# Stick-breaking attention: weights as differences of running products, or running products against differences of values

## The chip, the cores and the metric

One core of a Trainium2 chip runs the whole layer. The metric is the device time of one execution in microseconds; the time before is the median of three runs.

## What is computed

The layer has two branches, which are merged by gates, projected and normalised. The part that the change concerns is the attention, for 8 heads of width 64 and 1,024 positions:

```python
z = einsum('bthd,bshd->bhts', qb, kb) * scale
log_fail = where(causal, log_sigmoid(-z), 0.0)          # causal: s < t
later = cumsum(log_fail, axis=3, reverse=True) - log_fail
w = where(causal, exp(log_sigmoid(z) + later), 0.0)
outs.append(einsum('bhts,bshd->bthd', w, vb))
```

With beta = sigmoid(z), the weight of value s for query t is beta[t,s] times the product of (1 - beta[t,j]) over s < j < t. Let F[t,s] be the product of (1 - beta[t,j]) over s <= j < t, so that F[t,t] = 1. Then the weight is F[t,s+1] - F[t,s], and the sum over s of weight times value is also v[t] plus the sum over s <= t of F[t,s] times (v[s-1] - v[s]), with v[-1] = 0. The kernel before uses the first form, the kernel after the last.

The rest of the layer is an input projection of x (1,024 by 5,632), a convolution of width 31 with a layer norm, two projections of the branches, an output projection and a layer norm over the residual sum.

## The kernel before, in words

All products are float32 split into a high and a low part: each 128x128 by 512 product is three matmuls (`mm_piece`, L194 to L206: high by high, high by low, low by high). Weights arrive in pieces of 128x512 by SyncE's DMA queue (L284), and `split_weight` (L233) makes the two parts: ScalarE copies the high part (L235); the low part is made by VectorE (L237), by GpSimd (L239), or by a negated copy (L241) and an accumulating DMA of GpSimd's queue (L242).

The order of the instructions on every engine is worked out on the host, when the program is built, by a small planner, `Timeline` (L65). It holds a clock for TensorE and for the other engines, the cost of each operation, and a queue for each engine, from which the operation of the lowest priority number that is ready goes first. On the chip each engine runs its list in order and waits on semaphores. For DMAs the planner assumes fixed times: 3,000 ns for a load of 256 KB, 3,500 or 4,500 ns for larger ones, `W_LAND` = 3,000 ns after the issue of an accumulating one.

The stages, in order of TensorE's work:

1. The values v = x wv (L1145), all eight blocks of 128 positions at once in the eight banks of PSUM. `ev_v` (L1151) adds the bias into a half block `vraw` (VectorE), and splits it into `v` (ScalarE L1160, VectorE L1161). There are 128 positions on the partitions of each block.
2. The dense items (`run_dense`, L307) in the order of a hand-written list (L1073 to L1095): q and k of heads 0 and 1, the first pair of the convolution's inputs, q and k of 2 and 3, and so on. The attention (`Attention.step`, L827) is put between them: whatever it can do goes first, and dense matmuls fill the rest.
3. The pairs: ten pairs of dense columns by a seven-product scheme (`run_pairs`, L1023), with convolution and its layer norm on VectorE below them.
4. The branch projections (`ev_a`, `ev_c`), the output projection (L1292, L1307) and the final norm.

A unit of attention is a head and two blocks of 128 queries, with all keys before them. `emit_z` (L727) makes z in PSUM by two matmuls a chunk (L734, L735). ScalarE makes f = sigmoid(-z) (L742) and b = sigmoid(z) (L743). When a block of queries has all its chunks, VectorE runs a scan over f backwards (L749), which leaves F in f, with 1 on the diagonal from the constant `eyez`; then it multiplies b by F shifted by one (L752). The last column of b is set to zero by GpSimd (L724). `emit_t` (L758) transposes blocks of b on TensorE (L767), ScalarE and VectorE split the result into `wth` and `wtl` (L774, L775), and `emit_pv` (L781) multiplies them by the values (L790), with the high part of v in the first 64 rows of the result and the low part in the last 64. At the end of a unit ScalarE copies the low rows to `pvt` (L805), and VectorE adds both into the head pair's result `att` (L806). When both heads of a pair are done, the gate of the attention (`ev_zatt`, L430) multiplies `att`, which is stored to memory (`keep`, L444).

`slots` (L708) limits the blocks in work: at most `N_F` = 3 for f and `N_W` = 5 for b. The planner also counts the half blocks in use (`live["hf"]`, at most `N_HF` = 8), among them one for the bias `bvt` until the last block of v is done (L1165).

Of the kernel before, what the change touches and what calls it, by code (L numbers as in the profile page):

```python
# [14 lines left out]
P = 128  # L15
# [3 lines left out]
H = 8  # L19
# [14 lines left out]


N_BLK, N_HF, N_RAW, N_SPL = 43, 8, 2, 5

N_F, N_W = 3, 5

# [21 lines left out]

W_LAND = 3000


class Timeline:  # L65
# [5 lines left out]
    def __init__(self):  # L71
        self.t = 0.0
        self.free = {"A": 0.0, "V": 0.0, "G": 0.0}
        self.queue = {"A": [], "V": [], "G": []}
        self.events = []
        self.pe = deque()
        self.seq = 0
        self.now = 0.0

    def at(self, when, fn):  # L80
# [81 lines left out]
def layer_kernel(ctx: ExitStack, tc, xT, x, wv, wd, wa, wc, wo, vec, bv, lng, lnb, cst, out):  # L162
# [92 lines left out]
    def feed(loads=1 << 30):  # L255
        while True:
# [21 lines left out]
            if i < min(loads, len(pieces)):  # L278
                if isinstance(pieces[i], tuple):
                    stat["load"] += 1  # L280
                    continue
                if stat["raw"] < N_RAW:
                    r = wp.tile([P, HALF], F32, name=f"wr{i}", tag="wr", bufs=N_RAW)
                    nc.sync.dma_start(r, pieces[i])  # L284
                    raw[i] = (r, tl.t + 3000)
                    stat["load"] += 1
                    stat["raw"] += 1
                    continue
# [141 lines left out]
    def ev_zatt(p):  # L430
# [11 lines left out]
        return f  # L442

    def keep(key, src, cols=slice(0, S)):  # L444
# [3 lines left out]
        nc.sync.dma_start(kept[key][:, cols], src)  # L448
        n_kept[key] = n_kept.get(key, 0) + 1

    def back(key, name):
        t = blk(name)
        nc.sync.dma_start(t, kept[key])
        return t

    def split_att(p):
        a = back(("att", p), f"attb{p}")
        yield tl.now + 3500
# [59 lines left out]
    def make_cc(i):  # L518
# [3 lines left out]
        z = back(("c", ZCONV0 + i), f"zs{i}")  # L522
        yield tl.now + 3500
        cch[i], ccl[i] = blk(f"cch{i}", F32R), blk(f"ccl{i}", F32R)
# [182 lines left out]

    slots = {"f": 0, "w": 0}  # L708

    def alloc_unit(u):  # L710
        n = u.nslots
        ft = [blk(f"f{u.h}{u.m}{i}") for i in range(n)]
        bt = [blk(f"b{u.h}{u.m}{i}") for i in range(n)]
        slots["f"] += n
        slots["w"] += n
        if n == 1:
            u.f = [ft[0][:, 0:HALF], ft[0][:, HALF:S]]
            u.w = [bt[0][:, 0:HALF], bt[0][:, HALF:S]]
        else:
            u.f, u.w = [t[:, :] for t in ft], [t[:, :] for t in bt]  # L720
        for tb in range(2):

            last = P * (2 * u.m + tb + 1) - 1
            nc.gpsimd.memset(u.w[tb][:, last:last + 1], 0.0)  # L724
            tl.cost("G", tl.t, 0)

    def emit_z(u):  # L727
# [9 lines left out]
        c1 = min(c1, n)  # L737
        f, w = u.f[tb], u.w[tb]
        c2 = min(c1, n - 1)

        def g():
            yield act(0, f[:, c0:c1], ps[:, :c1 - c0], AF.Sigmoid, n=c1 - c0, scale=-SCALE)  # L742
            yield act(0, w[:, c0:c2], ps[:, :c2 - c0], AF.Sigmoid, n=c1 - c0, scale=SCALE)  # L743
            drop("ps")
            u.left[tb] -= 1
            if u.left[tb]:
                return

            yield ("V", 2, n, lambda: nc.vector.tensor_tensor_scan(  # L749
                f[:, 0:n][:, ::-1], f[:, 0:n][:, ::-1], eyez[:, S - n:S][:, ::-1], 0.0, op0=ALU.mult,  # L750
                op1=ALU.max), {"per": 2.083})
            u.ready[tb] = yield vtt(1, w[:, 0:n - 1], w[:, 0:n - 1], f[:, 1:n], ALU.mult, n)  # L752
            if u.nslots == 2 or u.ready[1 - tb] is not None:
                slots["f"] -= 1

        tl.spawn(g(), tl.t + 165)

    def emit_t(u):  # L758
# [22 lines left out]
    def emit_pv(u, i, wh, wl):  # L781
# [13 lines left out]
        if i == 0:  # L795
            p = h // 2
            if att[p] is None:
                att[p] = blk(f"att{p}")
            tmp = hf(f"pvt{h}{m}")
            r0 = (h % 2) * DH  # L800
            dst = att[p][r0:r0 + DH, m * 256:(m + 1) * 256].rearrange("p (b t) -> p b t", b=2)[:, ::-1, :]
# [18 lines left out]
    class Attention:  # L820
# [6 lines left out]
        def step(self):  # L827

            now = tl.t
            if self.pvq and self.pvq[0][0] is not None and self.pvq[0][0] <= now - GUARD and \  # L830
                    (self.pvq[0][1].ps is not None or live["ps"] < 7):
                emit_pv(*self.pvq.popleft()[1:])
                return True
            if self.zd and live["hf"] <= N_HF - 2 and live["ps"] < 7:
                u = self.zd[0]
                if all(r is not None and r <= now - GUARD for r in u.ready):
                    self.pvq.append(emit_t(u))
                    if not u.t:
                        self.zd.popleft()
                        slots["w"] -= u.nslots  # L840
                    return True
            if self.cur is None and self.wait:
                u = self.wait[0]
                if qk_ready[u.h] <= now and slots["w"] + u.nslots <= N_W and slots["f"] + u.nslots <= N_F:
                    self.cur = self.wait.popleft()
# [27 lines left out]
    def make_t(k):  # L873
# [3 lines left out]
        nc.sync.dma_start(rb, xT[k + NK // 2])  # L877
        yield tl.now + 4500
        a, b = blk(f"ta{k}"), blk(f"tb{k}")
# [21 lines left out]
    def make_s(n):  # L901
        c0, c1 = pairs[n]
        ra, rb = blk(f"rc{c0}"), blk(f"rc{c1}")
        nc.sync.dma_start(ra, wd[c0])
        nc.sync.dma_start(rb, wd[c1])
        while live["hf"] >= N_HF:
            yield tl.now + 200
        s = hf(f"s{n}")
        yield tl.now + 4500
        have = source[n] = {"A22": rb[:, hi_]}  # L910
# [19 lines left out]
    def split_operand(wh, wl, n, name, then):  # L930
# [4 lines left out]
        if name in DMA_LOW:  # L935
            yield act(1, wl, src, scale=-1.0)
            dsrc = wd[pairs[n][1]][:, hi_] if name == "A22" else src
            e = yield "G", 0, 0, lambda: nc.gpsimd.dma_start(wl, dsrc, accum_op=ALU.add), {"extra": 430}
            e += W_LAND
        else:  # L940
# [9 lines left out]
    def gate_out(t, c, half):  # L950
# [10 lines left out]
        keep(("c", c), t, cols)  # L961
        yield tl.now + 3000
        drop("hf")

    def pair_out(n, pp):
# [16 lines left out]
        nc.sync.dma_start(u, kept["p1", n][:, lo_])  # L982
        yield tl.now + 3000
        yield from add(u, "P6", u)
# [87 lines left out]

    qk_item(0)  # L1073
    qk_item(1)
    glu_item(0)
    qk_item(2)
    qk_item(3)
    glu_item(1)
    zatt_item(0)
    qk_item(4)  # L1080
    qk_item(5)
    zatt_item(1)
    qk_item(6)
    qk_item(7)
    p12_item(0)
    p12_item(1)
    zatt_item(2)
    att_done = lambda: flags["att"]
    z_done = lambda: heads_z_done(H - 1)
    glu_item(2, z_done)  # L1090
    glu_item(3, z_done)
    p12_item(2)
    zatt_item(3)
    for n in range(3, len(pairs)):
        p12_item(n)  # L1095
# [53 lines left out]
    tl.free["V"] = tl.t - 4000  # L1149

    def ev_v(tb):  # L1151
        while live["hf"] >= N_HF:
            yield tl.now + 100
        t = hf(f"vraw{tb}")
        vt[tb] = blk(f"v{tb}", F32R)
        v3 = vt[tb].rearrange("p (h e) -> p h e", h=H)
        t3 = t.rearrange("p (h e) -> p h e", h=H)
        yield vtt(0, t, vps[tb], bvt, ALU.add)
        drop("ps")
        yield "A", 0, HALF, lambda: nc.scalar.activation(v3[:, :, 0:DH], t3, AF.Copy)  # L1160
        yield "V", 1, HALF, lambda: nc.vector.tensor_tensor(v3[:, :, DH:P], t3, f32(v3[:, :, 0:DH]), op=ALU.subtract)  # L1161
        drop("hf")
        v_left[0] -= 1
        if v_left[0] == 0:
            drop("hf")  # L1165

# [10 lines left out]
    next(dense)  # L1177
    v_left = [NT]
    for tb in range(NT):
        tl.spawn(ev_v(tb), tl.t - (NT - 1 - tb) * 680 + 165)  # L1180
# [4 lines left out]
    def wo_stream():  # L1185
        for i in range(2 * NK):
# [5 lines left out]
            nc.sync.dma_start(r, src)  # L1192
            yield tl.now + 3000
            if i % 2 == 0:
# [198 lines left out]
```

## Time and profile before

| | |
|---|---|
| median of three runs | 768.82 us (767.13 to 770.05) |
| the profiled execution: its own time | 767.04 us |
| its span, first to last instruction | 765.0 us |
| TensorE busy | 748.2 us, 98% of the span |
| VectorE busy | 651.3 us, 85% |
| ScalarE busy | 379.7 us, 50% |
| GpSimd busy | 69.5 us, 9% |
| mean granted clock of TensorE | 0.994 |

A busy time is the time in which at least one instruction of the engine ran; the records of TensorE overlap, so its busy time says only when it stood still. A group's idle time is how long its engine stood idle just before its instructions, with what ended that wait. The DMA share of a stretch is the mean busy share of the core's 16 DMA engines.

### The profile page before, as it was taken

The page shows a single profiled execution, that of the slowest core. Times are in us where ns is not written, and L with a number is a line of the kernel's source. Part 1 is how long each engine was busy: PE and PEld are TensorE (multiplying, and loading weights), DVE is VectorE, ACT ScalarE, POOL GpSimd, SP SyncE. Part 2 cuts the span into 40 slices and gives each one's busy share as a digit, 9 for nine tenths or more (in the row PEclk, how much of TensorE's full clock was granted, in tenths as well). Part 3 has the DMA queues.
Part 4 walks back from the last instruction along what each step waited for, and adds up shares of the span by engine and source line. Part 5 has one row for each costly group of instructions (what it writes and reads, how often), then busy time and mean ns, then how long its engine had stood idle before and what let it go on. Part 6 is the DMA issues. An engine that isn't in the chain of part 4 may idle for free.

```text
span 765.0 us, 10211 instructions
## 1 busy us (share of the span) xinstructions
PE 748.2 (98%) x3622; PEld 625.4 (82%) x3622; DVE 651.3 (85%) x1006; ACT 379.7 (50%) x716; POOL 69.5 (9%) x132
## 2 busy tenths in 40 slices
PE   9999999999999999999999999999998999999995
PEld 7888888788888878888888888877786888888885
DVE  7554999999999999997999999999699859810985
ACT  2149965986388799844524433345472424200100
POOL 3311011101011011101100000000000023000000
PEclk9999999999999999999999999999999999999998
DMA  7525123412432224557725454453347876230052
GB/s 233 184 63 110 35 56 74 92 30 62 103 80 59 57 56 96 125 140 259 207 83 185 146 163 155 139 191 125 126 149 240 317 266 217 79 148 1 0 200 75
DMA packets 43394, 98.01 MB, mean 128 GB/s; under 512 B 4816, under 2 KB 5712, under 8 KB 43344
## 3 DMA queue, kind: packets, MB, share of 16 engines
q1 hardware_dynamic: 36864, 85.77, 33.5%
q0 software_dynamic: 6336, 11.54, 9.4%
q8 instruction: 28, 0.46, 0.3%
q14 instruction: 22, 0.18, 0.1%
q10 hardware_dynamic: 144, 0.07, 0.0%
HBM read 77.95 MB, written 19.40 MB: 127 GB/s over the span
## 4 chain that ended last, share of the span: by engine, by line
PE 58%; DVE 25%; ACT 9%; issue 6%; DMA 2%; SPq 0%; DVEq 0%; ACTq 0%
PE dps L203 11%; PE dps L198 11%; PE dps L199 11%; PE vps L1145 6%; DVE cacc L399 4%; PE yps L209 4%; PE yps L210 4%; PE yps L211 4%; PE pvps L790 3%; PE tps L767 3%; DVE cs L399 2%; DVE wl L396 2%; DVE c L396 2%; DVE cacc L396 2%; DVE u L396 2%
## 5 line engine op out<-in xcount | busy, mean ns | idle before, releaser
L198 PE MATMUL dps<-xh,wh 128*128 128x512 f32 x400 | 157.0, 393 | 0.0
L199 PE MATMUL dps<-xl,wh 128*128 128x512 f32 x400 | 156.0, 390 | 0.0
L203 PE MATMUL dps<-xh,wl 128*128 128x512 f32 x400 | 109.0, 391 | 0.0
L749 DVE TENSOR_TENSOR_SCAN f<-f,eyez 128x896 f32<-128x896 f32 (+3 forms) x64 | 85.0, 1343 | 5.1 <-ACT f L393 5.1
L235 ACT ACTIVATE wh<-wr 128x512 fp32r<-128x512 f32 x84 | 53.3, 634 | 72.4 <-DMA wr<-wv 25.5
L199 PEld LDWEIGHTS dps<-xl,wh 128*128 128x128 f32 x400 | 75.2, 188 | 14.2
L198 PEld LDWEIGHTS dps<-xh,wh 128*128 128x128 f32 x400 | 75.1, 188 | 14.3
L203 PEld LDWEIGHTS dps<-xh,wl 128*128 128x128 f32 x400 | 74.1, 188 | 14.6
L399 DVE SCALAR_TENSOR_TENSOR cacc<-cin,vecs,cacc 128x511 f32<-128x511 f32 (+14 forms) x116 | 82.4, 735 | 0.1
L242 POOL DMA_DIRECT2D wl<-wd x44 | 38.2, 868 | 271.7 <-ACT wl L241 240.8
L239 POOL TENSOR_TENSOR wl<-wr,wh 128x512 fp32r<-128x512 f32 x18 | 26.2, 1460 | 293.9 <-DVE wl L237 231.1
L210 PE MATMUL yps<-wol,mh 128*128 128x512 f32 (+1 forms) x136 | 51.2, 377 | 0.0
L211 PE MATMUL yps<-woh,ml 128*128 128x512 f32 (+1 forms) x136 | 51.2, 376 | 0.0
L209 PE MATMUL yps<-woh,mh 128*128 128x512 f32 (+1 forms) x136 | 51.2, 376 | 0.0
L396 DVE TENSOR_TENSOR wtl<-tps,wth 128x384 fp32r<-128x384 f32 (+1 forms) x80 | 46.7, 625 | 4.0 <-ACT wth L393 3.5
L399 DVE SCALAR_TENSOR_TENSOR xrow<-xrow,yps 128x512 f32<-128x512 f32 (+1 forms) x17 | 10.7, 653 | 43.0 <-PE yps L211 42.7
L393 ACT ACTIVATE f<-zps 128x384 f32<-128x384 f32 (+2 forms) x96 | 45.3, 515 | 3.8 <-PE zps L735 3.0
L393 ACT ACTIVATE wth<-tps 128x384 fp32r<-128x384 f32 (+1 forms) x80 | 40.2, 559 | 13.9 <-PE tps L767 13.2
L396 DVE TENSOR_TENSOR b<-b,f 128x895 f32<-128x895 f32 (+3 forms) x64 | 46.8, 743 | 0.3
L393 ACT ACTIVATE b<-zps 128x383 f32<-128x383 f32 (+2 forms) x96 | 46.2, 536 | 0.1
L399 DVE SCALAR_TENSOR_TENSOR cs<-cs,hs__77 128x511 f32<-128x511 f32 (+14 forms) x60 | 44.1, 735 | 0.1
L790 PE MATMUL pvps<-wtl,v 128*128 128x256 f32 (+1 forms) x160 | 39.7, 287 | 0.3 <-DVE wtl L396 0.2
(174 smaller groups left out, 1637.6 us busy)
## 6 DMA issues: line engine op xcount, KB each, us to landing
wr<-wd SPq DMA_DIRECT2D x60, 256.0 KB, 3.0
wl<-wd POOLq DMA_DIRECT2D x44, 256.0 KB, 4.6
rc<-wd SPq DMA_DIRECT2D x20, 512.0 KB, 5.6
c<-c SPq DMA_DIRECT2D x30, 256.0 KB, 3.1
ga<-c SPq DMA_DIRECT2D x8, 512.0 KB, 5.2
wor<-wo SPq DMA_DIRECT2D x16, 256.0 KB, 4.7
gc<-c SPq DMA_DIRECT2D x8, 512.0 KB, 6.3
xrow<-x SPq DMA_DIRECT2D x8, 512.0 KB, 5.8
```

Of the source, the lines that this page charges most:

```text
L198: nc.tensor.matmul(ps, wh[:, kk], mh, start=first and kk is ks[0], stop=False)
L199: nc.tensor.matmul(ps, wh[:, kk], ml, start=False, stop=False)
L203: nc.tensor.matmul(ps, wl[:, kk], mh, start=False, stop=last and kk is ks[3])
L209: nc.tensor.matmul(ps, wh, mh, start=first, stop=False)
L210: nc.tensor.matmul(ps, wh, ml, start=False, stop=False)
L211: nc.tensor.matmul(ps, wl, mh, start=False, stop=last)
L235: yield "A", 1, HALF, lambda: nc.scalar.activation(wh, r, AF.Copy)
L393: return "A", u, n, (lambda: nc.scalar.activation(out, in_, func, **kw)), (BIAS if "bias" in kw else {})
L396: return "V", u, n, lambda: nc.vector.tensor_tensor(out, a, b, op=op)
L399: return "V", u, n, (lambda: nc.vector.scalar_tensor_tensor(out, a, s, b, op0, op1)), (PTR if ptr else {})
L749: yield ("V", 2, n, lambda: nc.vector.tensor_tensor_scan(f[:, 0:n][:, ::-1], f[:, 0:n][:, ::-1], eyez[:, S - n:S][:, ::-1], 0.0, op0=ALU.mult,
L790: nc.tensor.matmul(u.ps[:, 0:n], st, wt[:, jj * 256:jj * 256 + n], start=(i == m and jj == 0 and wt is wh), stop=(i == 0 and jj == 1 and w ...
```

## The change

The kernel after transposes F itself, not b, and multiplies it by differences of values.

- In the attention: the second sigmoid, the multiplication by the shifted F and the zeroed column go. `N_F` becomes 6 and `N_W` goes. The scan's end is what the transposes wait for.
- In `ev_v`: the biased values stay in a block `vraw` (half t). A DMA of ScalarE's queue copies rows 0 to 126 of t to rows 1 to 127 of the other half, s; a second one brings the last row of the block before into row 0 (GpSimd sets a zero in the first block). TensorE transposes t in four matmuls, and four ScalarE copies put the result into `att`. VectorE makes s - t, which is then split as before. No value product is planned until all eight blocks are done.
- At the end of a unit ScalarE copies all 128 rows of the product to `pvt`, and two accumulating DMAs of GpSimd's queue add its two halves to `att`, one after the other (both write the same 64 rows).
- The planner gets one clock for all DMAs (`Timeline.dma`): each transfer takes its size at 250 bytes a ns after the ones before it, plus 2,000 ns; accumulating ones weigh 2.2 times. The copies of `ev_v` are not on that clock.
- The dense items follow a string, in which the convolution's third pair of inputs comes earlier (before the gate of head pair 1) and the fourth after the gate of pair 2; neither waits any more for all z to be done.
- The half block of `bvt` is no longer given back in the planner's count.

```diff
+ORDER = "q0 q1 g0 q2 q3 g1 z0 q4 q5 g2 z1 q6 q7 p2 z2 g3 p1 z3"
-N_F, N_W = 3, 5
+N_F = 6
-W_LAND = 3000
+DMA_RATE, W_ACC = 250, 2.2
...
+    def dma(self, kb, when=None, weight=1.0):
+        when = max(self.now, self.t) if when is None else when
+        self.dma_free = max(self.dma_free, when) + weight * kb * 1024 / DMA_RATE
+        return self.dma_free + 2000
...
-            e += W_LAND
+            e = tl.dma(256, e, W_ACC) + 500
...
-            yield act(0, w[:, c0:c2], ps[:, :c2 - c0], AF.Sigmoid, n=c1 - c0, scale=SCALE)
...
-            yield ("V", 2, n, lambda: nc.vector.tensor_tensor_scan(
+            u.ready[tb] = yield ("V", 2, n, lambda: nc.vector.tensor_tensor_scan(
...
-            u.ready[tb] = yield vtt(1, w[:, 0:n - 1], w[:, 0:n - 1], f[:, 1:n], ALU.mult, n)
...
-                    nc.tensor.transpose(ps[:, o:o + P], u.w[tb][:, j * P:(j + 1) * P], ident)
+                    nc.tensor.transpose(ps[:, o:o + P], u.f[tb][:, j * P:(j + 1) * P], ident)
...
-                yield act(0, tmp[0:DH, 0:256], u.ps[DH:P, 0:256], n=256)
-                yield vtt(0, dst, two(u.ps[0:DH, 0:256]), two(tmp[0:DH, 0:256]), ALU.add, 256)
+                yield act(0, two(tmp[:, 0:256])[:, ::-1, :], two(u.ps[:, 0:256]), n=256)
                 drop("ps")
+                for part in (slice(0, DH), slice(DH, P)):
+                    e = yield "G", 1, 0, (lambda part=part: nc.gpsimd.dma_start(dst, tmp[part, 0:256],
+                                                                                accum_op=ALU.add)), {"extra": 430}
+                    yield tl.dma(64, e, W_ACC) + 2000
...
+        vraw[tb] = b = blk(f"vraw{tb}")
+        t, s = b[:, 0:HALF], b[:, HALF:S]
+        yield vtt(0, t, vps[tb], bvt, ALU.add)
+        drop("ps")
...
+        nc.scalar.dma_start(s[1:P, :], t[0:P - 1, :])
+        if tb:
+            nc.scalar.dma_start(s[0:1, :], vraw[tb - 1][P - 1:P, 0:HALF])
+        else:
+            nc.gpsimd.memset(s[0:1, :], 0.0)
...
+            for p in range(NC):
+                nc.tensor.transpose(ps[:, p * P:(p + 1) * P], t[:, p * P:(p + 1) * P], ident)
...
+        yield [act(1, att[p][:, tb * P:(tb + 1) * P], ps[:, p * P:(p + 1) * P], n=P) for p in range(NC)]
+        drop("ps")
+        yield tl.now + 1500
...
+        yield vtt(1, s, s, t, ALU.subtract)
+        yield "A", 0, HALF, lambda: nc.scalar.activation(v3[:, :, 0:DH], s3, AF.Copy)
+        yield "V", 1, HALF, lambda: nc.vector.tensor_tensor(v3[:, :, DH:P], s3, f32(v3[:, :, 0:DH]), op=ALU.subtract)
         v_left[0] -= 1
-        if v_left[0] == 0:
-            drop("hf")
```

## Rows read from the trace of the kernel before

**Rows 1.** The page: busy time, share of the span and instructions of each engine.

```profile
PE 748.2 (98%) x3622; PEld 625.4 (82%) x3622; DVE 651.3 (85%) x1006; ACT 379.7 (50%) x716; POOL 69.5 (9%) x132
```

**Rows 2.** Stretches: us, busy us of PE, PEld, DVE, ACT, POOL; clock, DMA share, GB/s.

```profile
60.00:80.00 20.00, 19.84 (x103) 16.63 (x102) 11.98 (x15) 19.70 (x40) 3.91 (x14) 1.00 0.51 106
...
220.00:240.00 20.00, 19.46 (x108) 16.66 (x107) 19.76 (x26) 19.67 (x44) 2.20 (x8) 1.00 0.24 53
260.00:280.00 20.00, 19.02 (x112) 15.82 (x110) 18.22 (x27) 19.50 (x41) 2.07 (x8) 1.00 0.28 54
...
520.00:540.00 20.00, 18.63 (x90) 15.34 (x90) 17.39 (x26) 12.03 (x19) 0.00 (x0) 1.00 0.54 169
580.00:600.00 20.00, 17.48 (x67) 13.31 (x67) 15.56 (x24) 5.46 (x9) 0.00 (x0) 0.91 0.92 326
```

**Rows 3.** Groups by line that the change removes or replaces.

```profile
L396 DVE TENSOR_TENSOR b<-b,f 128x895 f32<-128x895 f32 (+3 forms) x64 | 46.8, 743 | 0.3
L393 ACT ACTIVATE b<-zps 128x383 f32<-128x383 f32 (+2 forms) x96 | 46.2, 536 | 0.1
L396 DVE TENSOR_TENSOR att<-pvps,pvt 64x256 f32<-64x256 f32 x32 | 12.7, 407 | 1.4 <-ACT pvt L393 0.9
L724 POOL MEMSET b<- 128x1 f32 x64 | 8.8, 390 | 16.1 <-PE tps L767 12.1 <-DVE b L396 4.0
```

**Rows 4.** Groups by line nearest to what the change adds.

```profile
L767 PE MATMUL tps<-eyez,b 128*128 128x128 f32 x288 | 37.3, 273 | 1.7 <-DVE b L396 1.6
L1338 ACT ACTIVATE xrow<-xrow,st 128x128 f32<-128x128 f32 x1 | 0.4, 387 | 0.0
L242 POOL DMA_DIRECT2D wl<-wd x44 | 38.2, 868 | 271.7 <-ACT wl L241 240.8 <-PE dps L203 12.0 <-ACT f L393 6.7
```

**Rows 5.** The tile vraw: duration min/median/max in ns, first and last start in us.

```profile
L396 DVE TENSOR_TENSOR vraw<-vps,bvt x8: 681/691/692, 45.0 to 50.9; 128x512 f32<-128x512 f32 x8
L1160 ACT ACTIVATE v<-vraw x8: 615/624/633, 45.7 to 51.6; 128x512 fp32r<-128x512 f32 x8
L1161 DVE TENSOR_TENSOR v<-vraw,v x8: 680/684/685, 49.7 to 54.5; 128x512 fp32r<-128x512 f32 x8
```

**Rows 6.** DMA queues: packets, MB, time as a share of 16 engines' span.

```profile
q1 hardware_dynamic: 36864, 85.77, 33.5%
q0 software_dynamic: 6336, 11.54, 9.4%
q10 hardware_dynamic: 144, 0.07, 0.0%
```

**Rows 7.** DMA issues by line: count, KB each, median us to landing.

```profile
wr<-wd SPq DMA_DIRECT2D x60, 256.0 KB, 3.0
wl<-wd POOLq DMA_DIRECT2D x44, 256.0 KB, 4.6
```

**Rows 8.** Stretches of 5 us after the values, columns as in the second group.

```profile
50.00:55.00 5.00, 5.00 (x23) 4.13 (x22) 5.00 (x9) 3.00 (x6) 1.88 (x2) 1.00 0.60 144
55.00:60.00 5.00, 5.00 (x24) 4.13 (x22) 0.94 (x2) 4.67 (x8) 0.86 (x1) 1.00 0.83 183
60.00:65.00 5.00, 5.00 (x24) 4.13 (x22) 0.75 (x1) 4.88 (x9) 1.92 (x6) 1.00 0.90 182
65.00:70.00 5.00, 5.00 (x25) 4.13 (x24) 2.02 (x1) 4.97 (x12) 0.00 (x0) 1.00 0.37 68
70.00:75.00 5.00, 5.00 (x23) 4.13 (x22) 4.20 (x5) 4.90 (x11) 0.85 (x1) 1.00 0.07 18
```

**Rows 9.** Timeline, 67 to 79 us: start us, us, engine, line, operation; idle before.

```profile
67.44 2.02 DVE L749 TENSOR_TENSOR_SCAN f<-f,eyez 128x896 f32<-128x896 f32 x1 [5.06 <-ACT f L393]
...
76.23 1.42 PE L767 MATMUL tps<-eyez,b 128*128 128x128 f32 x11 [0.15 <-DVE b L396]
...
78.55 0.28 PE L790 MATMUL pvps<-wth,v 128*128 128x256 f32 x1
```

**Rows 10.** The tile tps: duration min/median/max in ns, first and last start in us.

```profile
L767 PE MATMUL tps<-eyez,b x288: 270/273/328, 76.2 to 336.0; 128*128 128x128 f32 x144
```

More of the change, by code (lines that the diff above doesn't have):

```diff
@@ L448, in keep @@
         nc.sync.dma_start(kept[key][:, cols], src)
+        tl.dma((cols.stop - cols.start) / 2)
         n_kept[key] = n_kept.get(key, 0) + 1
@@ L457, in split_att @@
         a = back(("att", p), f"attb{p}")
-        yield tl.now + 3500
+        yield landed[f"attb{p}"]
         ach[p], acl[p] = blk(f"ach{p}", F32R), blk(f"acl{p}", F32R)
@@ L522, in make_cc @@
         z = back(("c", ZCONV0 + i), f"zs{i}")
-        yield tl.now + 3500
+        yield landed[f"zs{i}"]
         cch[i], ccl[i] = blk(f"cch{i}", F32R), blk(f"ccl{i}", F32R)
@@ L712, in alloc_unit @@
         ft = [blk(f"f{u.h}{u.m}{i}") for i in range(n)]
-        bt = [blk(f"b{u.h}{u.m}{i}") for i in range(n)]
         slots["f"] += n
[L715 to L725, printed above, removed]
+        u.f = [ft[0][:, 0:HALF], ft[0][:, HALF:S]] if n == 1 else [t[:, :] for t in ft]
     def emit_z(u):
@@ L829, in step @@
             now = tl.t
-            if self.pvq and self.pvq[0][0] is not None and self.pvq[0][0] <= now - GUARD and \
+            if v_left[0] == 0 and self.pvq and self.pvq[0][0] is not None and self.pvq[0][0] <= now - GUARD and \
                     (self.pvq[0][1].ps is not None or live["ps"] < 7):
@@ L843, in step @@
                 u = self.wait[0]
-                if qk_ready[u.h] <= now and slots["w"] + u.nslots <= N_W and slots["f"] + u.nslots <= N_F:
+                if qk_ready[u.h] <= now and slots["f"] + u.nslots <= N_F:
                     self.cur = self.wait.popleft()
@@ L877, in make_t @@
         nc.sync.dma_start(rb, xT[k + NK // 2])
-        yield tl.now + 4500
+        yield tl.dma(1024)
         a, b = blk(f"ta{k}"), blk(f"tb{k}")
@@ L908, in make_s @@
         s = hf(f"s{n}")
-        yield tl.now + 4500
+        yield max(e, tl.now)
         have = source[n] = {"A22": rb[:, hi_]}
@@ L961, in gate_out @@
         keep(("c", c), t, cols)
-        yield tl.now + 3000
+        yield tl.dma_free + 2000
         drop("hf")
@@ L982, in pair_out @@
         nc.sync.dma_start(u, kept["p1", n][:, lo_])
-        yield tl.now + 3000
+        yield tl.dma(256)
         yield from add(u, "P6", u)
@@ L1071, in p12_item @@
         add_item(wd_src(pairs[n][0]), None, ev_p12(n), lambda: True, 1)
[L1073 to L1094, printed above, removed]
+    p12 = iter(range(len(pairs)))
+    for what in ORDER.split():
+        n = int(what[1:])
+        if what[0] == "q":
+            qk_item(n)
+        elif what[0] == "g":
+            glu_item(n)
+        elif what[0] == "z":
+            zatt_item(n)
+        else:
+            for _ in range(n):
+                p12_item(next(p12))
+    for n in p12:
         p12_item(n)
@@ L1149, in layer_kernel, with turn @@
     tl.free["V"] = tl.t - 4000
+    vraw = {}
     def ev_v(tb):
-        while live["hf"] >= N_HF:
-            yield tl.now + 100
-        t = hf(f"vraw{tb}")
+        vraw[tb] = b = blk(f"vraw{tb}")
+        t, s = b[:, 0:HALF], b[:, HALF:S]
+        yield vtt(0, t, vps[tb], bvt, ALU.add)
+        drop("ps")
+        raw_there.add(tb)
+        while tb and tb - 1 not in raw_there:
+            yield tl.now + 100
+        nc.scalar.dma_start(s[1:P, :], t[0:P - 1, :])
+        if tb:
+            nc.scalar.dma_start(s[0:1, :], vraw[tb - 1][P - 1:P, 0:HALF])
+        else:
+            nc.gpsimd.memset(s[0:1, :], 0.0)
+        got = []
+        def turn():
+            ps = bank("tps")
+            for p in range(NC):
+                nc.tensor.transpose(ps[:, p * P:(p + 1) * P], t[:, p * P:(p + 1) * P], ident)
+            tl.t += 4 * 109
+            got.append(ps)
+        yield turn
+        ps = got[0]
+        yield [act(1, att[p][:, tb * P:(tb + 1) * P], ps[:, p * P:(p + 1) * P], n=P) for p in range(NC)]
+        drop("ps")
+        yield tl.now + 1500
         vt[tb] = blk(f"v{tb}", F32R)
         v3 = vt[tb].rearrange("p (h e) -> p h e", h=H)
[L1157 to L1161, printed above, removed]
-        drop("hf")
+        s3 = s.rearrange("p (h e) -> p h e", h=H)
+        yield vtt(1, s, s, t, ALU.subtract)
+        yield "A", 0, HALF, lambda: nc.scalar.activation(v3[:, :, 0:DH], s3, AF.Copy)
+        yield "V", 1, HALF, lambda: nc.vector.tensor_tensor(v3[:, :, DH:P], s3, f32(v3[:, :, 0:DH]), op=ALU.subtract)
         v_left[0] -= 1
-        if v_left[0] == 0:
-            drop("hf")
+    raw_there = set()
     for i in range(NC):
@@ L1178, in layer_kernel @@
     v_left = [NT]
+    for p in range(NC):
+        att[p] = blk(f"att{p}")
     for tb in range(NT):
@@ L1192, in wo_stream @@
             nc.sync.dma_start(r, src)
-            yield tl.now + 3000
+            yield tl.dma(256)
             if i % 2 == 0:
```

21 lines of the change are left out of this document (10 added, 11 removed).

## The prediction

> **What bounds the kernel now.** I read the busy times first, then the stretches of 20 us, then the groups that the change touches. The reader is to see one thing in the first: TensorE is busy for 748.2 of 765.0 us [rows 1], so what VectorE and ScalarE save is worth time only where it ends a wait of TensorE. The stretches show how little of that there is. Of the 27 stretches between 60 and 600 us, ten hold idle time of TensorE of 0.05 us or more, the first at 60 to 80 and the last at 580 to 600, 6.8 us in all; the two largest outside the attention are 1.4 us at 520 to 540 and 2.5 us at 580 to 600, the latter with the granted clock at 0.91 (in part at 1.2 instead of 2.4 GHz), which costs 20 x 0.09 = 1.8 us more [rows 2]. So 8.6 us is about what can be won by taking waits away. The start, the output projection and the tail are not touched.
>
> The second thing is the stretch from 45 to 79 us. The values come out of PSUM from 45.0 us on and are split by 55.2 [rows 5]; the first scan starts at 67.4, the first transpose at 76.2, and the first value product at 78.6 [rows 9]. Some 23 us lie between the values being there and being wanted. VectorE is nearly idle in the middle of it, ScalarE is full from 55 on, and the DMA engines are 60 to 90% busy from 50 to 65 [rows 8]. The changed kernel puts its new steps here.
>
> **The change, part by part.**
>
> *Removed from the attention.* 96 second sigmoids, 46.2 us of ScalarE; 64 multiplications, 46.8 us, and 32 additions, 12.7 us, of VectorE; 64 memsets of GpSimd, 8.8 us [rows 3]. All of it lies beside TensorE's work. What it gives is shorter waits: the transposes' own waits for the multiplication are 1.6 us [rows 4], and VectorE, freed of 46.8 + 12.7 = 59.5 us less the 5.4 below, reaches the convolution's norm some 54 us sooner, so that this norm no longer competes with the operand splits before 540 and 600. I take the 5.7 us there (1.4 + 2.5 + 1.8) as won, and half of the other 2.9: 7.2 us. The bounds are 0 and 8.6.
>
> *Added to TensorE.* 8 x 4 transposes of t. 288 such cost 37.3 us of busy time [rows 4], 0.13 us each: 32 x 0.13 = 4.1 us, wholly on the path, since TensorE is the bound. The number of other matmuls is the same. Without the step below, the sum is 767.0 - 7.2 + 4.1 = 763.9 us.
>
> *Added to ScalarE and VectorE at the values.* 32 copies of 128 columns at up to 0.39 [rows 4], 12.4 us of ScalarE, and 8 differences at 0.68, 5.4 us of VectorE. ScalarE is full from 55 to 75 us [rows 8]; the copies take the place of about a quarter of the second sigmoids and delay q and k by a few us. I cost it at nothing because the four dense items ahead of heads 2 and 3, 4 x 48 matmuls at about 23 in 5 us [rows 8], are 42 us of work that stands ready; if it ran out, it would cost at most the 12.4.
>
> *Added to GpSimd's queue.* 64 accumulating DMAs, 64 x 0.87 = 56 us of issue [rows 4]. The second of each pair writes what the first writes and has to wait for its landing, 4.6 us where 256 KB are added [rows 7], and up to 32 x 4.6 = 147 us of that queue is waiting. The accumulations of weights stand behind it. Their pieces are split five ahead, so I cost it at nothing, and its failure is a rival. The planner's new DMA clock, the new order of the dense items and the half block that is not given back move no work of TensorE; I cost them at nothing within the bounds above.
>
> *The shift of the values.* This is the term that decides. Eight copies move 127 rows of 2 KB each from partition p to p + 1, on ScalarE's DMA queue, and VectorE's differences wait for them. No row shows such a copy. The lower bound is a load of 256 KB: 3.0 us [rows 7], hidden in the 23 us. For the upper bound, the queues' packets tell how rows are dealt: SyncE's queue has 256 transfers of 36,864 / 256 = 144 packets, which is 128 rows and one more for each of 16 engines; GpSimd's 44 have 6,336 / 44 = 144, and the one transfer of ScalarE's queue has 144 [rows 6]. So every transfer of this trace deals 8 whole rows to each of 16 engines. 127 rows can be dealt in equal whole shares only to one engine. If that is what happens, the rate is that of one engine: 85.77 MB in 0.335 x 16 x 765 = 4,100 us, 20.9 KB a us [rows 6]. Eight copies are 8 x 127 x 2,048 bytes = 2.08 MB, so 99.5 us on one engine, one behind the other.
>
> I take the upper end: the row nearest in size has 128 rows, but equal shares are what all 301 transfers show, and 127 has no other. The Trainium skill, on its page "DMA: Bandwidth & Descriptors" (section "Why a DMA increments its semaphore by 16 and not by 1"), says that a transfer runs on the largest number of engines up to 16 that divides the outer count of both sides, and names 127 partitions as a case of one; no run here shows it. The same page gives about 27 GiB/s for an engine, which would make the eight copies an estimated 72 us and my total about 819; the rows decide for the slower rate.
>
> Then the sum is this. The first copy can start when the first addition ends, 45.0 + 0.7 = 45.7 us [rows 5]. The engine also carries its share of the loads, by the DMA shares of 50 to 75 us 5 x (0.60 + 0.83 + 0.90 + 0.37 + 0.07) = 13.9 us [rows 8]; after that TensorE stands, and no more is asked for. The last copy lands at 45.7 + 99.5 + 13.9 = 159.1; difference, copy and low part take 0.68 + 0.62 + 0.68 [rows 5], so the values are there at 161.1. The first value product wants the last blocks, and wanted them at 78.6 [rows 9]. TensorE stands for 82.5 us. Nothing hides it: the list of TensorE is fixed, and VectorE, whose differences stand ahead of the scans and of the later heads' q, stands too and cannot work ahead. Total 763.9 + 82.5 = 846.4 against the profiled execution's own 767.0, which lies 1.8 below the median of the runs shown; within the width of this sum I leave that out and say 846.
>
> The bounds: at the fastest mean rate of any stretch shown, 326 / (16 x 0.92) = 22.1 KB a us [rows 2], and without other traffic, the values are there at 45.7 + 94.2 + 2.0 = 141.9, which makes 763.9 + 63.3 = 827; with the trace's mean share of traffic, 33.5 + 9.4 = 43% [rows 6], over all 100 us instead of the 13.9, they are there at 190 and the total is 875.
>
> **The rivals.**
>
> *The shift is spread over the engines* (0.29). Then it lands some 3 us after its issue, within the 23 us, and the total is 763.9, on the median's scale 766, with 758 to 773 for the bounds of idle time won (8.6 or 0). For it: the 3.0 us of the rows; nothing says that shares must be equal, a remainder could be dealt as well. Against it: no transfer in the trace has unequal shares. The same page of the Trainium skill reports an exception, rows dealt in rounded-up shares to all engines, for direct copies of GpSimd's queue; this copy is on ScalarE's. This case decides the sign: it holds if the copy lands within about 25 us for all eight, that is, on four engines or more.
>
> *The accumulations on GpSimd's queue are the wait* (0.06). The shift is quick, but each pair holds the queue for 0.87 + 4.6 + 0.87 = 6.3 us, 32 of them for 203 us of the 260 us of attention [rows 10], and the weights' low parts come up to 4.6 us late in places. If two or three of these land on TensorE, 764 + 9 to 14 = 773 to 778.
>
> *The shift is on one engine, and the first wait comes sooner* (within my case): if loads behind the copies are held up, TensorE stands from about 65 us on, some 14 us more than summed: 860.
>
> **How the numbers follow.** One engine: 0.65, forecast 846, its own range 825 to 875. Spread: 0.29, of which about half lies more than 0.5% below the median (0.5%, 3.8 us, is what a measurement of this kernel can tell from no change) and half within. GpSimd's queue: 0.06, slower for the most part. So faster 0.16, same 0.14, slower 0.70. Since both signs hold much of the chance, the range that holds 8 in 10 takes in most of the spread case: 760 to 875.
>
> **What would show it.** If I am right: in the DMA issues, the copies of vraw on ScalarE's queue take 12 us and more to land, the later ones near 100; in the waits, VectorE's difference (line of the helper, tile vraw) waits for that DMA some ten us at a time; a stretch between 75 and 150 us with hardly any TensorE; after it the stages as before. If the copies land in a few us and TensorE stays at 90% or more from 60 to 340 us, the rival holds and my forecast is wrong by the whole 82.5 us. VectorE's busy time falls by some 54 us either way, and 320 transposes take the place of 288. In the spread case the idle time at 520 to 600 should be gone; if it is still there, the freed time of VectorE was not what that wait wanted.

## The result, and the profile after

The kernel after takes 846.5 us (median of four runs, 845.22 to 847.30), the kernel before 767.98 in the same comparison: 1.1022 times as long, with an interval of 1.0985 to 1.1059. The forecast was 846. The total is right, but partly by luck: several of its terms are wrong and happen to cancel, and the wait begins on another engine and 24 us earlier than I said. The profiled execution took 847.3 us, against 767.04 of the one before.

The page of the kernel after, busy times and DMA queues, answers to [rows 1, 6]:

```profile
PE 756.6 (90%) x3654; PEld 631.9 (75%) x3654; DVE 605.4 (72%) x918; ACT 350.4 (41%) x652; POOL 118.1 (14%) x133
...
q1 hardware_dynamic: 36864, 85.77, 29.7%
q0 software_dynamic: 11456, 15.74, 12.7%
q10 hardware_dynamic: 1392, 2.16, 0.7%
```

The last row decides the term that was open. ScalarE's queue had 144 packets before and has 1,392 now. The seven one-row copies have 224, 32 each (the run below with the shift on GpSimd's queue leaves 368 = 144 + 224 here): by this count 16 engines, each with one packet of data and one that closes. What is left for the eight shift copies is 1,392 - 144 - 224 = 1,024, or 128 each: 127 rows and a single closing packet. Each shift copy ran on one engine.

Stretches of the kernel after, columns as in [rows 2]: the last of the values, the standstill, and what follows.

```profile
50.00:55.00 5.00, 4.66 (x38) 4.17 (x36) 1.89 (x3) 0.00 (x0) 0.00 (x0) 1.00 0.06 22
...
70.00:80.00 10.00, 0.00 (x0) 0.00 (x0) 0.69 (x1) 0.00 (x0) 0.00 (x0) 0.50 0.07 26
...
110.00:120.00 10.00, 0.00 (x0) 0.00 (x0) 0.00 (x0) 0.00 (x0) 0.00 (x0) 0.50 0.07 26
120.00:126.00 6.00, 0.00 (x0) 0.00 (x0) 0.00 (x0) 0.00 (x0) 0.00 (x0) 0.50 0.07 26
126.00:130.00 4.00, 3.05 (x7) 2.47 (x8) 0.00 (x0) 3.89 (x23) 0.00 (x0) 0.50 0.08 28
130.00:135.00 5.00, 5.00 (x17) 3.93 (x17) 4.85 (x9) 5.00 (x19) 0.00 (x0) 0.72 0.05 21
134.00:135.00 1.00, 1.00 (x6) 0.82 (x5) 1.00 (x3) 1.00 (x6) 0.00 (x0) 1.00 0.01 4
```

A DMA share of 0.07 is 1/16: one engine busy, fifteen idle, 26 KB a us, for as long as nothing else runs; the last copy is through at about 134 us. The four compute engines do next to nothing until 126. The granted clock falls to 0.50 (1.2 GHz) after TensorE has stopped, and stays there for the first matmuls after it.

Who waited for whom on TensorE (waits; us in total, times, longest), and ScalarE's and TensorE's timelines at both ends of the standstill:

```profile
PE dps L207 <- ACT att L402: 72.3, 1, 72.3
PE dps L212 <- DVE wl L246: 3.2, 2, 2.4
PE tps L764 <- DVE f L749: 2.0, 3, 0.9
```

```profile
47.16 1.87 ACTq L1156 DMA_DIRECT2D vraw<-vraw  x2
49.06 11.09 ACTq L1158 DMA_DIRECT2D vraw<-vraw  x1
...
116.13 0.61 ACTq L1156 DMA_DIRECT2D vraw<-vraw  x1
116.78 9.28 ACTq L1158 DMA_DIRECT2D vraw<-vraw  x1
126.11 3.50 ACT L402 ACTIVATE att<-tps 128x128 f32<-128x128 f32 x20 [32.20 <-issue]
```

```profile
51.00 3.65 PE L1167 MATMUL tps<-eyez,vraw 128*128 128x128 f32 x32
...
126.95 0.79 PE L207 MATMUL dps<-xh,wh 128*128 128x512 f32 x1 [72.29 <-ACT att L402]
127.54 0.63 PE L208 MATMUL dps<-xl,wh 128*128 128x512 f32 x1
```

L1156 issues the shift copies, L1158 the one-row copies. TensorE's wait here is not for landed data: it ends 7 us before the last copy is through. ScalarE's list holds the issues and its copies of the transposed values (att, L402) in one order, and the issue of each one-row copy takes 9 to 11 us. A shift copy is still issued in 0.6 us while another is moving; the issue behind it is held for about as long as a copy takes. It is the queue that holds it, not the engine that the rows share: SyncE's issues of the same one-row copies, on its own queue, took 0.5 us (a run below). TensorE has all eight PSUM banks taken by transposes that nobody copies out, and stops at 54.6 us.

The account of the 80.3 us between the two profiled executions: 72.3 of standing; some 2.8 at the lower clock (thirteen matmuls some 0.43 us apart until 132.7 us instead of 0.227); 3.7 for the 32 new transposes; 1.5 are left over. The freed time of VectorE (605.4 against 651.3 us busy, 45.9 less where I had said some 54) brought nothing: from 140 us on the stretches of 20 us hold 6.6 us of idle time of TensorE up to the end of the pairs, where the kernel before had 6.8.

### The profile page after: what moved, and what is told of

Read it like the earlier page. It is cut to its first block, busy times and chain, and to the rows that moved or that the text cites. A ratio compares the mean times of both kernels' runs of the same rounds, so it can differ in the third digit from the quotient of the medians.

```text
span 845.3 us, 10164 instructions
## 1 busy us (share of the span) xinstructions
PE 756.6 (90%) x3654; PEld 631.9 (75%) x3654; DVE 605.4 (72%) x918; ACT 350.4 (41%) x652; POOL 118.1 (14%) x133
## 3 DMA queue, kind: packets, MB, share of 16 engines
q10 hardware_dynamic: 1392, 2.16, 0.7%
## 4 chain that ended last, share of the span: by engine, by line
PE 65%; DVE 18%; ACTq 8%; DMA 4%; ACT 3%; issue 2%; POOL 1%; DVEq 0%; SPq 0%; POOLq 0%
PE dps L212 9%; PE dps L207 9%; PE dps L208 9%; ACTq L1158 7%; DVE cacc L408 6%; PE sps L207 5%; PE sps L208 5%; PE sps L212 5%; PE vps L1136 5%; PE yps L220 3%; PE yps L218 3%; PE yps L219 3%; PE pvps L787 3%; DVE cs L408 3%; DVE f L749 3%; PE tps L764 3%
## 5 line engine op out<-in xcount | busy, mean ns | idle before, releaser
L207 PE MATMUL dps<-xh,wh 128*128 128x512 f32 x400 | 161.5, 404 | 72.4 <-ACT att L402 72.3
L208 PE MATMUL dps<-xl,wh 128*128 128x512 f32 x400 | 158.2, 395 | 0.0
L212 PE MATMUL dps<-xh,wl 128*128 128x512 f32 x400 | 113.0, 398 | 3.6 <-DVE wl L246 3.2
L749 DVE TENSOR_TENSOR_SCAN f<-f,eyez 128x896 f32<-128x896 f32 (+3 forms) x64 | 83.0, 1339 | 5.6 <-ACT f L402 5.6
L248 POOL TENSOR_TENSOR wl<-wr,wh 128x512 fp32r<-128x512 f32 x18 | 24.5, 1369 | 296.9 <-ACT wh L244 296.9
L804 POOL DMA_DIRECT2D att<-pvt x64 | 55.8, 1021 | 64.9 <-ACT pvt L402 50.0
L402 ACT ACTIVATE wth<-tps 128x384 fp32r<-128x384 f32 (+1 forms) x80 | 42.5, 555 | 36.6 <-PE tps L764 35.8
L764 PE MATMUL tps<-eyez,f 128*128 128x128 f32 x288 | 42.1, 275 | 2.0 <-DVE f L749 2.0
L1181 DVE TENSOR_TENSOR v<-vraw,v 128x512 fp32r<-128x512 f32 x8 | 5.4, 686 | 48.7 <-ACT v L1180 48.7
L787 PE MATMUL pvps<-wth,v 128*128 128x256 f32 (+1 forms) x160 | 40.1, 275 | 0.0
```

The costliest lines, as they stand in the source:

```text
L207: nc.tensor.matmul(ps, wh[:, kk], mh, start=first and kk is ks[0], stop=False)
L208: nc.tensor.matmul(ps, wh[:, kk], ml, start=False, stop=False)
L212: nc.tensor.matmul(ps, wl[:, kk], mh, start=False, stop=last and kk is ks[3])
L749: u.ready[tb] = yield ("V", 2, n, lambda: nc.vector.tensor_tensor_scan(f[:, 0:n][:, ::-1], f[:, 0:n][:, ::-1], eyez[:, S - n:S][:, ::-1], ...
L764: nc.tensor.transpose(ps[:, o:o + P], u.f[tb][:, j * P:(j + 1) * P], ident)
L787: nc.tensor.matmul(u.ps[:, 0:n], st, wt[:, jj * 256:jj * 256 + n], start=(i == m and jj == 0 and wt is wh), stop=(i == 0 and jj == 1 and w ...
```

## The experiments

**The shift in two copies, 112 and 15 rows.** The question is whether the 127 rows are the cause.

```diff
-        nc.scalar.dma_start(s[1:P, :], t[0:P - 1, :])
+        nc.scalar.dma_start(s[1:113, :], t[0:112, :])
+        nc.scalar.dma_start(s[113:P, :], t[112:P - 1, :])
```

> The shift of each value block is cut into two copies, 112 rows and 15 rows; nothing else changes. Theory A (127 rows are dealt to one DMA engine, and what stands behind them on ScalarE's queue waits until that engine has taken them): 112 rows deal 7 to each of 16 engines, the one-row copies issue in about 0.6 us instead of 9.8, TensorE's 72 us of standing still are gone, and the total is 764 to 774. Theory B (the one-row copies, or the new transposes and copies on ScalarE, are what holds the queue): the one-row copies still take 9 to 11 us each and the total stays at 840 to 850.

784.83 us, 1.0242 (1.0219 to 1.0265) times the kernel before. The one-row issues fall from 9.8 to 0.56 us as theory A said, and theory B falls; but the total misses A's 774 by 11 us. The tile vraw (durations in ns, first and last start in us) and TensorE's longest wait tell why; the queue's packets follow:

```profile
L1156 ACTq DMA_DIRECT2D vraw<-vraw x8: 518/545/616, 47.4 to 62.9; - x8
L1157 ACTq DMA_DIRECT2D vraw<-vraw x8: 838/839/1367, 48.0 to 63.5; - x8
...
L1159 ACTq DMA_DIRECT2D vraw<-vraw x7: 558/564/1095, 51.0 to 64.3; - x7
```

```profile
PE dps L207 <- ACT att L402: 10.9, 1, 10.9
```

```profile
q10 hardware_dynamic: 1632, 2.16, 0.9%
```

23 issues at 0.55 to 0.84 us keep ScalarE's list from 47.4 to 64.9 us, so its copies of the values start 14 us after the transposes and TensorE stands for 10.9 us, then runs at the lower clock. The planner gives an issue on ScalarE no time at all. I had left this term out. The packets are 144 + 224 + 8 x 158, and 158 is (112 + 16) + (15 + 15): 16 engines and 15.

**The shift in 122 and 5 rows.** If equal shares of whole rows are the rule, 122 rows go to two engines.

```diff
-        nc.scalar.dma_start(s[1:P, :], t[0:P - 1, :])
+        nc.scalar.dma_start(s[1:123, :], t[0:122, :])
+        nc.scalar.dma_start(s[123:P, :], t[122:P - 1, :])
```

> The shift is cut into 122 rows and 5 rows. Theory A, if equal shares of whole rows are the rule: 122 rows deal to two engines, 61 each, so the eight copies take half of 80 us, TensorE stands still for some 32 to 36 us instead of 72, and the total is about 805 to 812; the DMA share while TensorE stands is about 0.12 instead of 0.07. If unequal shares were dealt: as with 112 and 15, below 775. Theory B: 840 to 850.

805.64 us. TensorE's wait, the queue's packets and two stretches of the standstill:

```profile
PE dps L207 <- ACT att L402: 31.6, 1, 31.6
```

```profile
q10 hardware_dynamic: 1440, 2.16, 0.8%
```

```profile
76.00:78.00 2.00, 0.00 (x0) 0.00 (x0) 0.00 (x0) 0.00 (x0) 0.00 (x0) 0.50 0.14 54
78.00:80.00 2.00, 0.00 (x0) 0.00 (x0) 0.00 (x0) 0.00 (x0) 0.00 (x0) 0.50 0.14 52
```

1,440 - 144 - 224 = 1,072 packets, 134 for each pair of copies: (122 + 2) + (5 + 5), two engines and five. The share is 2/16 and the rate twice 26 KB a us. Half the rows per engine, somewhat less than half the wait (31.6 us for 72.3): the wait follows the rows that one engine has to move.

**The shift on GpSimd's queue.**

```diff
-        nc.scalar.dma_start(s[1:P, :], t[0:P - 1, :])
+        nc.gpsimd.dma_start(s[1:P, :], t[0:P - 1, :])
```

> The 127-row copies are issued by GpSimd's queue instead of ScalarE's, the one-row copies stay on ScalarE's. If GpSimd's queue deals rounded-up shares of 127 rows to 16 engines (the exception on the Trainium skill's page DMA: Bandwidth & Descriptors): landing in 3 to 5 us, one-row copies issued in 0.6 us, total 764 to 776. If it deals them to one engine too: the copies land 10 us apart, VectorE's differences wait, and the total is 810 to 850.

773.11 us, 1.0082 (1.0055 to 1.0110). The queue's packets, the issues (median us to landing), the shift's issues and VectorE's differences (tile vraw), and what TensorE waits for then:

```profile
q0 software_dynamic: 12096, 17.82, 14.8%
```

```profile
vraw<-vraw POOLq DMA_DIRECT2D x8, 254.0 KB, 5.5
```

```profile
L1156 POOL DMA_DIRECT2D vraw<-vraw x8: 530/552/936, 45.8 to 52.1; - x8
L405 DVE TENSOR_TENSOR vraw<-vraw x8: 680/684/693, 50.2 to 61.6; 128x512 f32<-128x512 f32 x8
```

```profile
PE dps L212 <- DVE wl L246: 3.7, 2, 2.4
PE tps L764 <- DVE f L749: 2.0, 3, 0.9
```

The last difference starts at 61.6 us, 15.8 us after the first issue, so that the 2.08 MB moved at 132 KB a us or more, five times the 26 of one engine: the rows were spread. The queue has 640 packets more than in the kernel after, 80 a copy, which fits 16 engines with a closing packet each, but does not count the engines by itself. The Trainium skill, on its page "DMA: Bandwidth & Descriptors" (section "Why a DMA increments its semaphore by 16 and not by 1"), gives an exception for some direct copies of GpSimd's queue, whose rows go to all 16 engines in rounded-up shares; that the rows were spread agrees with it. The same 127 rows cost 73 us less. So the form of the attention, freed of its stall, is still 6.5 us slower than the kernel before (766.57 in that comparison), where my spread case had 766.

**The one-row copies on SyncE's queue.**

```diff
-            nc.scalar.dma_start(s[0:1, :], vraw[tb - 1][P - 1:P, 0:HALF])
+            nc.sync.dma_start(s[0:1, :], vraw[tb - 1][P - 1:P, 0:HALF])
```

> The 127-row copies stay on ScalarE's queue, the one-row copies go to SyncE's. Theory A: the eight copies still need 80 us of one engine, until about 127 us; whether ScalarE is free or not, TensorE cannot have its values before then, so the total is 820 to 848; SyncE's issues of the one-row copies (or ScalarE's of the next 127-row ones) are now the long ones. Theory B, if the one-row copies are dear by themselves on ScalarE's queue: the total falls below 780.

847.93 us: no gain, as theory A said. Now the shift copies themselves are the long issues (tile vraw); the queue's packets, TensorE's two longest waits, and a step each of VectorE's and ScalarE's timelines follow:

```profile
L1156 ACTq DMA_DIRECT2D vraw<-vraw x8: 613/10080/12132, 47.1 to 104.1; - x8
...
L1158 SPq DMA_DIRECT2D vraw<-vraw x7: 497/527/1243, 47.1 to 94.1; - x7
```

```profile
q10 hardware_dynamic: 1168, 2.15, 0.7%
```

```profile
PE dps L207 <- ACT att L402: 60.4, 1, 60.4
PE zps L736 <- ACT qhh L402: 11.4, 1, 11.4
```

```profile
138.70 0.69 DVE L405 TENSOR_TENSOR vraw<-vraw 128x512 f32<-128x512 f32 x1 [12.17 <-DMA vraw<-vraw]
...
139.42 0.63 ACT L1180 ACTIVATE v<-vraw 128x512 fp32r<-128x512 f32 x1 [11.65 <-DVE vraw L405]
```

The first two issues take 2.1 us together, the other six 64: whatever comes next on the queue pays. With the shift copies alone on it, the queue has 144 + 8 x 128 packets, which confirms the count above. ScalarE is through with its issues 12 us sooner than in the kernel after, and TensorE starts again at 115.1 us. But then VectorE's last difference waits 12.17 us for its copy to land, ScalarE's parts of q stand behind it, and TensorE stands for another 11.4 us. So the landed data is a second limit, close behind the issues: 60.4 + 11.4 us take the place of 72.3. The shift copies on SyncE's queue, which would take all of these issues from ScalarE and leave only this second limit, were not run.

**The copies alone, in the kernel before.** Nothing reads what they write.

```diff
         t = hf(f"vraw{tb}")
+        s = blk(f"shift{tb}")
...
         yield vtt(0, t, vps[tb], bvt, ALU.add)
+        nc.scalar.dma_start(s[1:P, 0:HALF], t[0:P - 1, :])
```

> The kernel before, with the eight 127-row copies of the biased values on ScalarE's queue added, into blocks that nothing reads. Theory A: one DMA engine takes them one after the other, ScalarE's list stands behind the issue of the next, TensorE waits for ScalarE: some 55 to 75 us more than before, 822 to 842 (the eighth copy's own landing hides behind nothing that waits for it). Rival, that VectorE's wait for the landed values is what costs the time: nobody reads these, so 766 to 772.

829.44 us, 61.2 more than the kernel before (768.22 in that comparison). The issues of the copies (tile shift), and TensorE's waits:

```profile
L1160 ACTq DMA_DIRECT2D shift<-vraw x8: 614/10092/12049, 45.7 to 100.1; - x8
```

```profile
PE dps L198 <- ACT wh L235: 33.3, 2, 30.5
PE dps L203 <- DMA wl<-wd: 14.1, 1, 14.1
PE zps L734 <- ACT qhh L393: 8.5, 1, 8.5
```

Eight copies whose data no instruction reads cost nearly four fifths of the whole change (one addition of VectorE waited 8.4 us for a half block that a copy was still reading, while TensorE had work). The weight that TensorE waits 14.1 us for is late by ScalarE too, which made its negated copy only at 100.6 us. This is the cleanest reading of the case: ScalarE held at its issues is enough to cost the time, with no reader of the data; the run before it shows that VectorE's wait for the data stands close behind.

**Why the spread form is not faster.** Four further runs look at the 6.5 us. The kernel with the shift on GpSimd's queue loses the waits at 520 to 600 us as I forecast, and has new ones at 400 to 430, where the dense items' last weights are split among the operands of the pairs. Stretches of it:

```profile
400.00:420.00 20.00, 16.14 (x67) 12.32 (x66) 20.00 (x30) 9.06 (x13) 0.00 (x0) 0.97 0.47 168
420.00:440.00 20.00, 20.00 (x83) 15.86 (x82) 20.00 (x33) 9.11 (x16) 0.00 (x0) 0.94 0.51 178
...
580.00:600.00 20.00, 20.00 (x90) 16.57 (x89) 15.07 (x24) 6.07 (x11) 0.00 (x0) 1.00 0.64 226
```

First, the planner's clock against the fixed times (the others of the diff above are put back in the same way):

```diff
-            e = tl.dma(256, e, W_ACC) + 500
+            e += 3000
...
-                    raw[i] = (r, tl.dma(256))
+                    raw[i] = (r, tl.t + 3000)
...
-        yield tl.dma(1024)
+        yield tl.now + 4500
```

> As e3_gpsimd, with the planner's DMA times of the kernel before (fixed ones) in place of the one clock. Theory A says that the planner's clock only moves waits: 768 to 778, the same as e3_gpsimd's 773.1 within 5. Rival: the clock is what costs the 6.5 us that e3_gpsimd is above the kernel before: 764 to 769.

775.37 us, 1.0110 (1.0067 to 1.0153) times the kernel before: no gain. The waits at 400 to 430 are gone and the old kind is back at 460 to 480 (1.1 us) and 540 to 560 (3.1 us and a clock of 0.91). The clock moves the waits.

Second, the half block of the bias given back to the planner's count:

```diff
         v_left[0] -= 1
+        if v_left[0] == 0:
+            drop("hf")
```

> As e3_gpsimd, with the bias's half block given back in the planner's count when the values are done, as before. If seven half blocks instead of eight starve the attention or the pairs, the total falls by 2 us or more (771 or less); theory A, in which TensorE's list is full either way, says 773 within 2.

773.71 us, no difference that the runs can tell; no cost of that part of the change shows.

Third, the low parts of the last 14 weights from GpSimd:

```diff
-N_TURN, T_LOW = 14, "V"
+N_TURN, T_LOW = 14, "G"
```

> As e3_gpsimd, with the low parts of the last 14 weight pieces ahead of the pairs made by GpSimd instead of VectorE. e3_gpsimd has lost the waits at 580 to 600 us and has new ones of 3.9 us and a slower clock at 400 to 430, where TensorE waits for VectorE's low part of a weight that stands among the splits of the transformed x. If VectorE's crowding there is the cause: that wait goes, and the total is 767 to 770. If the weights are late for another reason (their loads): it stays, and the total is 772 to 778.

786.50 us, worse by 13 us, outside both expectations. TensorE no longer waits for VectorE's low parts but for ScalarE's high parts, 14.3 us in eight waits. An operation of GpSimd on a half block took 1.46 us in the kernel before against VectorE's 0.68, so this run put a slower step in the place of a late one and does not tell the two causes apart.

Fourth, the clock at a rate nearer to the chip's:

```diff
-DMA_RATE, W_ACC = 250, 2.2
+DMA_RATE, W_ACC = 330, 2.2
```

> As e3_gpsimd, with the planner's clock at 330 bytes a ns instead of 250 (the trace moved up to 326 KB a us). Theory A: the waits at 400 to 430 us, which the fixed times of e6_fixed_times did not have there, come from the clock reckoning the loads of that stretch too late, so that VectorE's low parts of weights stand too far back in its list. Then they shrink, and the total is 767 to 771. Rival: they come from the new order of the dense items; then they stay, and the total is 772 to 778.

765.40 us, 0.9984 (0.9972 to 0.9996), a little below both expectations. The stretch has no wait left, and neither has the one at 580 to 600:

```profile
400.00:420.00 20.00, 20.00 (x90) 16.55 (x89) 19.95 (x31) 9.53 (x15) 0.00 (x0) 1.00 0.59 198
420.00:440.00 20.00, 20.00 (x90) 16.55 (x89) 20.00 (x33) 9.72 (x17) 0.00 (x0) 1.00 0.47 153
...
580.00:600.00 20.00, 20.00 (x90) 16.55 (x89) 12.79 (x21) 5.64 (x10) 0.00 (x0) 1.00 0.71 234
```

So the rate that the planner reckons with makes that wait (the runs in the kernel before, below, say the same). That it orders VectorE's low parts too late, because it takes the loads of that stretch to be slower than they are, fits (the stretch before it, 360 to 380, moved 264 to 288 KB a us in these runs), but is argued, not shown.

**The other parts of the change, without the new attention.** The new order of the dense items alone, in the kernel before (the diff of ORDER shown above):

> The kernel before with the new order of the dense items alone (third and fourth pair of the convolution's inputs earlier, no waiting for all z). If the order by itself costs nothing: 765 to 771. If it takes away the dense work that covers the time between the attention's end and the pairs: 771 to 778.

770.76 us, 1.0039 (1.0017 to 1.0060): some 3 us, at the upper end of "costs nothing". There is no wait at 400 to 430 in it, so the order is not what makes that one; it has waits at 560 to 600 and 660 to 680.

The new order and the clock at 250, in the kernel before:

```diff
-W_LAND = 3000
+DMA_RATE, W_ACC = 250, 2.2
...
-            e += W_LAND
+            e = tl.dma(256, e, W_ACC) + 500
...
-                    raw[i] = (r, tl.t + 3000)
+                    raw[i] = (r, tl.dma(256))
```

> The kernel before with the new order and the planner's one clock for all DMAs, without the new form of the attention: the other part of the change alone. If the clock with its 250 bytes a ns is what makes the wait at 400 to 430: 770 to 776, with that wait there. If the clock helps: 762 to 767.

767.64 us, 1.0005 (0.9985 to 1.0025): below the expected 770 to 776, though the wait came where it was expected (3.4 us and a clock of 0.91 at 400 to 420); the waits at 580 to 600 are gone, and the two cancel.

The same with 330 in the place of 250:

> As e12_before_order_clock with the clock at 330 bytes a ns. If a better reckoning of the loads takes away the waits of the kernel before at 520 to 600 us (5.7 us with the slower clock) and puts none elsewhere: 761 to 766, below both kernels. If waits only move: 766 to 774.

759.81 us, 0.9906 (0.9886 to 0.9927), below both kernels and a little below the expected 761 to 766. All waits of TensorE that the profile shows:

```profile
PE tps L780 <- DVE b L405: 1.8, 3, 0.7
PE vps L1126 <- DVE ones L228: 1.1, 1, 1.1
PE pvps L803 <- ACT wth L402: 0.8, 1, 0.8
PE vps L1150 <- DVE xh L1141: 0.5, 1, 0.5
PE pvps L803 <- DVE wtl L405: 0.4, 2, 0.2
```

With the same order and clock, the old attention takes 759.81 and the new one, with its shift spread, 765.40: 5.6 us more. With the clock at 250 it is 767.64 and 773.11, 5.5 more, though from two comparisons. 3.7 of these are the 32 transposes (tile vraw, from 51.00 for 3.65 us above). At 330 another 0.9 is idle time of TensorE in the stretches from 60 to 600 us (4.3 against 3.4, most of the difference at 60 to 80, where the products that make z wait for ScalarE); the last us was not traced to a step.

## Why the prediction came out right, and where it did not

- *127 rows are dealt to one engine*: right, shown by the packets (128 a copy), by the share of 0.07, and by the runs with 122 rows, with 112 and 15, and with GpSimd's queue. The rule of the Trainium skill's page "DMA: Bandwidth & Descriptors" (section "Why a DMA increments its semaphore by 16 and not by 1"), the largest number up to 16 that divides the rows, fits all cases seen on ScalarE's queue: 127 on 1, 122 on 2, 112 on 16, 15 on 15, 5 on 5.
- *99.5 us for the copies, and 13.9 of other traffic*: too long. I took the mean rate of loads that share the engines, 20.9 KB a us; one engine alone moved 254 KB in about 10 us, 26 KB a us, and with everything standing there was little other traffic. The copies were through at about 134 us, not 159. The figure of about 27 GiB/s for an engine that the Trainium skill gives on the same page (section "Specifications"), 29 KB a us, was nearer than my row.
- *TensorE stands from 78.6 us, when the first value product is wanted*: wrong. It stood from 54.6. I had named VectorE's differences as the instructions that wait, and had costed ScalarE's new work at nothing; in truth ScalarE is held at the issue of the DMA behind each shift copy, with the copies that empty PSUM behind it. The run with the copies alone shows that this needs no reader of the data. The wait that I had named exists, but only as the second limit: it cost TensorE 11.4 us where the issues ended sooner. My rival within the case, a wait from 65 us on because things behind the copies are held up, was nearer, though it named the loads.
- These errors put the end of the standstill 34 us too late (161.1 for 126.95: 25 by the rate and the traffic, the rest because TensorE starts again with dense work before the values are there) and its start 24 too late, which leaves 72.3 for my 82.5; the lower clock after it, which I had not put into the sum, adds 2.8. The 7.2 us below, which were not won, make up for that. That the total came out at 846 is luck; that one engine moves all the rows is not.
- *7.2 us won by the freed time of VectorE*: wrong in its effect. The waits at 520 to 600 us did go where the shift was spread, but with the clock at 250 as many came at 400 to 430; only at 330 are both gone. And it was not the freed time that took them away: with the planner's clock they are gone in the old attention too, whose VectorE is as busy as before (651.7 and 651.3 us), and with the fixed times the new attention still has 3.1 us at 540 to 560. From 250 to 330 the old attention gains as much (7.8 us) as the new one (7.7).
- *4.1 us for the transposes*: 3.65 measured.
- *GpSimd's queue as a wait*: the second of each pair waited 8.6 us in all, 2.0 at most, with a landing of 2.8 us where I had taken 4.6; of TensorE's waits 0.3 us are for a weight that this queue adds. At nothing, as costed.
- *The spread case at 766*: 773.1, 7 above my centre and just outside its range (758 to 773). Without the stall the change would have been slower too, by 0.8% (with the shift on GpSimd's queue). So even had the rows been spread, my chances there leaned to the wrong side.

## What to carry to other kernels

Count the rows of a DMA between partitions before counting its bytes: 127 rows, a number with no divisor from 2 to 16, went to one engine here, and 254 KB then took 10 us, where 112 rows (224 KB) on 16 engines landed in 2.7. An issue on a compute engine's queue is work of that engine: on ScalarE 0.55 to 0.84 us each when the way is free, and about as long as a copy takes when copies ahead on that queue are not through, with everything in that engine's list behind it. Where TensorE is 98% busy, look for time in the waits that the plan itself makes (here a DMA rate of 250 bytes a ns where up to 326 were moved) before rebuilding a stage to free another engine.

## What the runs showed that I had not expected

- An issue of a DMA held ScalarE for 9.3 to 11.1 us while copies ahead on its queue were moving on one engine; the first two shift copies went out in 1.9 us together, and SyncE's one-row issues at the same time took 0.5 us each. How many rows may be outstanding on a queue before that happens was not tried.
- An issue of 15 rows on 15 engines took 0.84 us, one of 112 rows on 16 engines 0.55.
- After the standstill TensorE ran at 1.2 GHz from 126.95 to about 132.7 us.
- A better reckoned DMA clock in the host's planner, with the order of the dense items, is worth 0.94% on the kernel before (759.81 us); the change's own setting, 250, is worth nothing there (767.64).
